# GELU MLP on one core: the first W1 column group plain, W1 cast by GpSimd's queue, W2 through DRAM in fp16

## Chip, core and metric

One core of one Trainium2 chip. The metric is the device time of one execution in microseconds; lower is better. Inputs and output are fp32 in DRAM; the matmuls run in fp16 with fp32 sums in PSUM.

## Reference

```python
x = np.random.randn(16, 512, 768)     # seen as 8192 rows of 768
w1 = np.random.randn(768, 3072); b1 = np.random.randn(3072)
w2 = np.random.randn(3072, 768)

y = np.matmul(x, w1) + b1
y = 0.5 * y * (1.0 + erf(y / np.sqrt(2.0)))
return np.matmul(y, w2)
```

## The kernel before

**Two phases.** Phase 1 computes gelu(x W1 + b1) and stores it in fp16, transposed (hidden column on the partitions), in sixteen DRAM tensors `gd`, one for each 512 rows of x. Phase 2 reads `gd` back, multiplies by W2 and writes the output.

**Plain and fast products.** Both phases use a bilinear scheme of 20 block products where the ordinary product needs 24. The lists at the top (`P1_ORD`, `P1_WOPS`, `P1_XOPS`, `P1_OPS`, and those of `P2`) say which sums of blocks are multiplied and how the products are combined. In phase 1 a unit is one column group of W1 (512 of the 3072 columns, two halves of K by four tiles of 128) times one block of 1536 rows of x (three thirds of 512): 20 products of three matmuls. `w1_ops` makes the 20 operands of one W1 group (sums, differences and signed copies), `x_sums` makes the 13 sums of x of one block. There are five blocks and six groups, so 30 units; `p1_block(b)` runs the six units of one block. While a product is summed in PSUM, ScalarE copies and VectorE adds (L343, L348) take intermediate values out; a Gelu on ScalarE (L497, in `finish`) ends each output tile of 128 x 512, 12 a unit. In phase 2 a unit is 512 rows times all of W2: 20 products of eight matmuls with 384 columns (L873), 16 units.

The first 512 rows of x, which don't fit in blocks of 1536, go through `plain_tile`: six matmuls for one tile of 128 columns (L630), 24 tiles.

**Start.** x's first 512 rows and all six W1 groups come on SP's queue in fp32 (L396, L419) and are cast to fp16 by ScalarE and VectorE; the x tiles are transposed on TensorE (L480, evicted at L486 and L488). The 24 plain tiles follow. Next to three of them (`X1_AT`) GpSimd's queue loads the three thirds of block 0 (L643), with a cast on the way; they too are transposed on TensorE, and then block 0's units begin.

**x of later blocks.** `load_x(b)` has GpSimd's queue cast 256 rows at a time from x to a DRAM copy `xd` in fp16 (L667, six a block), and SP's queue load them with a transposing DMA (L671, six a block). The lists `CAST_AT` and `TR_AT` name the units of the block before behind which they are planned.

**Stores of Gelu.** Each Gelu writes into one of `NGST` = 11 staging slots; a DMA stores it to `gd` (L503: SP's queue, GpSimd's for 16 of the plain tiles), and the slot is free when the store has landed. In phase 2 the same memory holds `NOSB` output slots of 1536 bytes: 7.

**W2.** During the last block of phase 1, GpSimd's queue loads W2 in two halves with a cast (L772, four DMAs each, one buffer for both), and VectorE, GpSimd and ScalarE make the operands (`P2_WOPS`). Eight operands that are plain blocks of W2 are loaded once more, directly to where they stay (L810); these places are free only as the last units of phase 1 finish with W1's operands there.

**What sets the order.** The kernel schedules itself. `S.add` hands a task with its engines and guessed durations, the values that it reads, the buffer it allocates, `after=` (tasks that it is planned behind) and `due=` (a planned time) to `Sched`, which simulates the engines and emits every engine's instructions in the order that the simulation finds. TensorE's order is that of the code. An engine's queue is then worked off in that order, with waits where data or buffers need them.

Of the kernel before, what the change touches and what calls it, by code (L numbers as in the profile page):

```python
# [13 lines left out]
P = 128  # L14
# [24 lines left out]
X1_AT = (9, 12, 15)  # L39
# [213 lines left out]
def kernel(  # L253
# [21 lines left out]
    NS = 18  # L275
# [6 lines left out]
    NGST = 11  # L282
# [11 lines left out]
    xd = drp.tile([R, K], FP16, name="xd")  # L294

    def a16(off, n):
        return ar[:, off // 2: off // 2 + n]
# [4 lines left out]
    def s_off(i):  # L302
        return O_SUM + i * SL
# [50 lines left out]
    ctx.enter_context(tc.manual_schedule())  # L354
    make_identity(nc, ident[:])
# [18 lines left out]
    sums = Pool([s_off(i) for i in (16, 17)], heir=sums_done)  # L374
    xnat = Pool([s_off(14)], heir=lambda t, s: [sums.put(t, s + SL * i) for i in range(2)])
    xtr = Pool([s_off(12)], heir=lambda t, s: [sums.put(t, s + SL * i) for i in range(2)])
    wraw = Pool([s_off(i) for i in range(12)], heir=sums.put)
# [31 lines left out]
    w1load = []  # L409
    for u in range(6):  # L410
        halves = []
        cuts = ((0, 256), (256, 512)) if u == 0 else ((0, 512),)
        raw = [Val(wraw), Val(wraw)]
        done = [[None] * 4 for _ in range(2)]
        for c0, c1 in cuts:
            for i in range(2):
                o = O_WF + (u * 2 + i) * 6144
                f = Val()
                w1load.append(S.add({"SP": 0.45}, lambda e, o=o, i=i, c0=c0, c1=c1, u=u: nc.sync.dma_start(  # L419
                    out=a32(o, 1536).rearrange("p (k c) -> p k c", c=512)[:, :, c0:c1],  # L420
                    in_=w1r[:, 3 * i:3 * i + 3, u * 512 + c0:u * 512 + c1]), makes=[f], work=2.15 * (c1 - c0) / 512))
# [9 lines left out]
        wv.append((raw, done))  # L431
# [14 lines left out]
    def w1_ops(u, due):  # L446
        raw, done = wv[u]
        after = list(x0c) + (w1cast[:4 + 2 * u] if u else [])
# [173 lines left out]
    plain_mm = []  # L622

    def plain_tile(u, q):
        raw, done = wv[u]
        bv = Val(bank)

        def mm(e):
            for kc in range(KC):
                nc.tensor.matmul(out=ps[:, bv.slot, :], lhsT=raw_w1(u, 2 * q + kc // 3)[:, kc % 3, :],  # L630
                                 rhs=a16(x0T.slot + kc * 1024, 512), start=(kc == 0), stop=(kc == KC - 1))
        plain_mm.append(S.add({"PE": 6 * MM1}, mm, reads=[done[0][q], done[1][q], x0T], frees=[x0T, raw[0], raw[1]], alloc=bv))
        return finish(([bv], lambda: ps[:, bv.slot, :]), u * 4 + q, 0, 1, [bv], queue="POOL" if u < 4 else "SP")

    pg = []
    x1n = []
    for u in range(6):
        for q in range(4):
            pg.append(plain_tile(u, q))
            if u * 4 + q in X1_AT:  # L640
                j = len(x1n)
                v = Val()
                S.add({"POOL": 0.8}, lambda e, j=j: nc.gpsimd.dma_start(  # L643
                    out=a16(O_XB + j * 6144, 3072).rearrange("p (s k) -> p s k", k=K), in_=xr[:, 4 + 4 * j:8 + 4 * j, :]),
                    makes=[v], work=5.3, after=[pg[-1]])
                x1n.append(v)
    x1done = []
    for s in range(12):
        j, c = divmod(s, 4)
        pt, dur, ev, bv, dv = transpose_tile(  # L650
            x1n[j], lambda kc, s=s: a16(O_XB + s * 1536 + kc * 256, P),
            lambda j=j, c=c: x_third(0, j)[:, :, c * P:(c + 1) * P], xsv[0][j])
        x1done.append(pt)
        S.add(dur, ev, reads=[bv], makes=[xsv[0][j], xsv[0][3 + j]])
# [5 lines left out]
    def load_x(b):  # L660
        r0 = BLK[b]
        for y in range(6):
# [8 lines left out]
            S.add({"SP": 0.45}, lambda e, a=a, z=z, j=j: nc.sync.dma_start_transpose(  # L671
# [3 lines left out]
    def x_sums(b, due0, dur):  # L675
# [11 lines left out]
        for (d, op, a, z) in sorted(P1_XOPS, key=lambda o: (need[o[0]], o[0])):  # L687
# [4 lines left out]
            def fn(e, fa=fa, fb=fb, v=v, op=op):  # L692
                step = 1536 if e == "DVE" else 512
                for h in range(0, 1536, step):
                    comb(e, a16(v.slot + 2 * h, step), op, fa()[:, h:h + step], fb()[:, h:h + step])
            prev = [S.add({"DVE": dve_tt(1536), "POOL": 3 * pool_tt(512)} if b else {"DVE": dve_tt(1536)}, fn, reads=[va, vb], alloc=v,
                          order=prev, due=due0 + dur * need[d], port=True)]
# [3 lines left out]
    def p1_block(b):  # L701
# [4 lines left out]
        for u in range(6):  # L706
            if b == 0:
                w1_ops(u, S.pe_ideal - 1.0)

# [218 lines left out]
```

## Time and profile before

| | |
|---|---|
| median of 3 runs | 922.49 us (921.5 to 922.61) |
| profiled execution | 921.39 us, span 919.6 us |
| TensorE busy | 861.4 us (94%), 4601 matmuls |
| VectorE, ScalarE, GpSimd busy | 629.1, 430.4, 164.8 us |
| phase 2 matmuls (L873) | 2560, 419.3 us |
| phase 1 fast matmuls (L714) | 1800, 399.2 us |
| plain matmuls (L630) | 144, 33.2 us |
| direct W2 loads (L810), issue to landing | median 20.3 us |
| x casts to DRAM (L667), issue to landing | median 10.9 us |
| mean granted TensorE clock | 0.981 |

Times in the timeline run from the span's start. A row of the timeline has start, duration, engine, line, operation, names and count; in brackets stands the idle time of the engine before it and what ended that. Rows marked SPq are DMA issues, which don't count as busy. A stretch of TensorE's idle time is time that the kernel could lose; idle time of another engine is none in itself.

### The profile page before, as it was taken

The page shows a single profiled execution, that of the slowest core. Times are in us where ns is not written, and L with a number is a line of the kernel's source. Part 1 is how long each engine was busy: PE and PEld are TensorE (multiplying, and loading weights), DVE is VectorE, ACT ScalarE, POOL GpSimd, SP SyncE. Part 2 cuts the span into 40 slices and gives each one's busy share as a digit, 9 for nine tenths or more (in the row PEclk, how much of TensorE's full clock was granted, in tenths as well). Part 3 has the DMA queues.
Part 4 walks back from the last instruction along what each step waited for, and adds up shares of the span by engine and source line. Part 5 has one row for each costly group of instructions (what it writes and reads, how often), then busy time and mean ns, then how long its engine had stood idle before and what let it go on. Part 6 is the DMA issues. An engine that isn't in the chain of part 4 may idle for free.

```text
span 919.6 us, 13541 instructions
## 1 busy us (share of the span) xinstructions
PE 861.4 (94%) x4601; PEld 449.8 (49%) x4601; DVE 629.1 (68%) x1041; ACT 430.4 (47%) x711; POOL 164.8 (18%) x165
## 2 busy tenths in 40 slices
PE   6958999999899999987976999999999999999997
PEld 2433444444344444433433556565666666666664
DVE  4937567565656756678686677777777877777773
ACT  8856786787687768755763111212121111212121
POOL 1400085048007504645130000000000000000000
PEclk9979999999999999999999899999999999999999
DMA  9994747854874785482989655555665555555611
GB/s 336 274 214 120 190 138 160 229 162 146 209 189 144 171 218 161 126 196 73 200 254 297 185 173 185 166 176 169 206 206 191 165 172 190 167 164 190 206 69 69
DMA packets 132793, 166.85 MB, mean 181 GB/s; under 512 B 47580, under 2 KB 121332, under 8 KB 126196
## 3 DMA queue, kind: packets, MB, share of 16 engines
q1 hardware_dynamic: 122144, 144.22, 49.7%
q0 software_dynamic: 10544, 21.76, 12.7%
q8 instruction: 36, 0.59, 0.3%
q14 instruction: 33, 0.27, 0.1%
q10 hardware_dynamic: 36, 0.01, 0.0%
HBM read 100.68 MB, written 84.93 MB: 202 GB/s over the span
## 4 chain that ended last, share of the span: by engine, by line
PE 82%; DMA 7%; DVE 6%; ACT 3%; issue 2%; SPq 0%; POOL 0%; ACTq 0%; DVEq 0%; POOLq 0%
PE ps L873 44%; PE ps L714 35%; DVE ar L343 4%; DMA gd<-ar 4%; DMA ar<-in_w_dram 3%; PE ps L630 2%; DVE vt L343 2%; ACT ar L488 1%; ACT ar L497 1%; ACT ar L348 1%; ACT vt L348 1%; SPq L396 0%; DVE ar L352 0%; SPq L419 0%; ACT L497 0%
## 5 line engine op out<-in xcount | busy, mean ns | idle before, releaser
L873 PE MATMUL ps<-ar 128*128 128x384 f16 x2560 | 419.3, 327 | 8.9 <-DMA ar<-in_w_dram 8.9
L714 PE MATMUL ps<-ar 128*128 128x512 f16 x1800 | 399.2, 383 | 28.0 <-DVE vt L343 19.1
L873 PEld LDWEIGHTS <-ar 128*128 128x128 f16 x2560 | 250.8, 98 | 177.4 <-issue 9.9
L714 PEld LDWEIGHTS <-ar 128*128 128x128 f16 x1800 | 177.1, 99 | 249.9 <-issue 42.1
L343 DVE TENSOR_TENSOR vt<-vt,ps 128x512 f32<-128x512 f32 (+1 forms) x260 | 167.6, 645 | 139.2 <-ACT vt L348 70.4
L343 DVE TENSOR_TENSOR ar<-ar 128x1024 f16<-128x1024 f16 (+2 forms) x385 | 248.9, 674 | 20.2 <-PE ps L873 9.8
L348 ACT ACTIVATE vt<-ps 128x512 f32<-128x512 f32 (+1 forms) x232 | 125.1, 542 | 263.1 <-PE ps L873 238.1
L497 ACT ACTIVATE ar<-vt,b1t 128x512 f16<-128x512 f32 x240 | 166.5, 717 | 93.4 <-DVE vt L343 83.8
L343 DVE TENSOR_TENSOR vt<-ps,vt 128x512 f32<-128x512 f32 (+1 forms) x230 | 147.5, 642 | 77.9 <-ACT vt L348 34.5
L343 POOL TENSOR_TENSOR ar<-ar 128x512 f16<-128x512 f16 (+1 forms) x98 | 129.1, 1352 | 254.5 <-PE ps L714 126.8
L497 ACT ACTIVATE ar<-ps,b1t 128x512 f16<-128x512 f32 x144 | 93.1, 675 | 10.9 <-DMA gd<-ar 9.3
L348 ACT ACTIVATE ar<-vt 128x384 f32<-128x384 f32 x48 | 25.1, 523 | 109.7 <-DVE vt L343 77.9
L630 PE MATMUL ps<-ar 128*128 128x512 f16 x144 | 33.2, 392 | 2.7 <-ACT ar L348 1.7
L341 DVE SCALAR_TENSOR_TENSOR vt<-vt,ps 128x512 f32<-128x512 f32 (+1 forms) x46 | 29.3, 637 | 3.7 <-PE ps L714 0.8
L348 ACT ACTIVATE ar<-ar 128x1536 f16<-128x1536 f32 (+4 forms) x30 | 27.7, 953 | 6.2 <-DMA ar<-in_w_dram 4.9
L343 DVE TENSOR_TENSOR ar<-vt 128x384 f32<-128x384 f32 x48 | 26.8, 559 | 1.7
L630 PEld LDWEIGHTS <-ar 128*128 128x128 f16 x144 | 14.3, 100 | 21.4 <-ACT ar L348 2.8
L341 DVE SCALAR_TENSOR_TENSOR ar<-vt,ps 128x384 f32<-128x384 f32 x16 | 8.9, 554 | 22.0 <-PE ps L873 22.0
L480 PE MATMUL ps<-ident,ar 128*128 128x128 f16 x96 | 9.8, 270 | 10.5 <-DMA ar<-in_x_dram 7.7
L503 POOL DMA_DIRECT2D gd<-ar x16 | 8.8, 556 | 30.6 <-ACT ar L497 30.6
L480 PEld LDWEIGHTS <-ar 128*128 128x128 f16 x96 | 7.5, 120 | 12.7 <-DMA ar<-in_x_dram 8.1
L667 POOL DMA_DIRECT2D xd<-in_x_dram x24 | 11.7, 494 | 5.5 <-DMA ar<-in_x_dram 5.5
(23 smaller groups left out, 57.4 us busy)
## 6 DMA issues: line engine op xcount, KB each, us to landing
ar<-gd SPq DMA_DIRECT2D x48, 1024.0 KB, 5.5
gd<-ar SPq DMA_DIRECT2D x368, 128.0 KB, 1.8
out_dram<-ar SPq DMA_DIRECT2D x128, 192.0 KB, 2.0
xd<-in_x_dram POOLq DMA_DIRECT2D x24, 384.0 KB, 10.9
ar<-in_w_dram SPq DMA_DIRECT2D x10, 768.0 KB, 13.2
ar<-in_w_dram POOLq DMA_DIRECT2D x8, 576.0 KB, 11.4
ar<-in_w_dram POOLq DMA_DIRECT2D x8, 384.0 KB, 20.3
ar<-in_x_dram POOLq DMA_DIRECT2D x3, 768.0 KB, 10.0
```

What stands on the lines that cost most here:

```text
L341: eng.scalar_tensor_tensor(out=o, in0=a, scalar=-1.0, in1=b, op0=ALU.mult, op1=ALU.subtract)
L343: eng.tensor_tensor(out=o, in0=a, in1=b, op=ALU.add if op == "+" else ALU.subtract)
L348: nc.scalar.activation(out=o, in_=a, func=ACTF.Copy, scale=float(sg))
L480: nc.tensor.transpose(out=o[:, kc * P:(kc + 1) * P], in_=nat_ap(kc), identity=ident[:])
L488: nc.scalar.copy(out=dst_fn(), in_=i)
L497: ft = S.add({"ACT": act_ps(512) + 0.02}, lambda e: nc.scalar.activation(out=a16(g.slot, 512), in_=src[1](), func=ACTF.Gelu, bias=b1t[:, t ...
L503: {"SP": nc.sync, "POOL": nc.gpsimd}[e].dma_start(out=gd[un][:, t, :], in_=a16(g.slot, 512))
L630: nc.tensor.matmul(out=ps[:, bv.slot, :], lhsT=raw_w1(u, 2 * q + kc // 3)[:, kc % 3, :], rhs=a16(x0T.slot + kc * 1024, 512), start=(kc == ...
L667: S.add({"POOL": 0.5}, lambda e, a=a: nc.gpsimd.dma_start(out=xd[a:a + 256, :], in_=xf[a:a + 256, :]), makes=[c], work=2.1, after=gate)
L714: nc.tensor.matmul(out=ps[:, bk, :], lhsT=w1_ap(u, w)[:, kt * P:(kt + 1) * P], rhs=xa[:, kt * 512:(kt + 1) * 512], start=(first and kt == ...
L873: nc.tensor.matmul(out=ps[:, bk, 0:NB], lhsT=xa[:, j, :], rhs=a16(w2half[w][j // 4].slot + (j % 4) * W1T, NB), start=(first and j == 0), s ...
```

## The change

- The first W1 group is computed plain for block 0 as well (with all of its rows, so 2048 rows of that group are plain); block 0 keeps five fast units. Groups 1 and 2 are plain for the first 512 rows before the fast units, groups 3 to 5 each just before their own unit.
- Only group 0 of W1 is loaded in fp32 by SP. Groups 1 to 5 are loaded with a cast by GpSimd's queue, two DMAs a group, into four slots that are used again. Block 0's x is loaded by the same queue, in turn with groups 1 and 2.
- W2 is cast into a DRAM copy `w2d` by four DMAs on GpSimd's queue, planned behind units 3 and 4 of blocks 1 and 2. The loads of W2 (both halves and the direct ones) read `w2d` on SP's queue.
- The transposing loads of x are issued by ScalarE's queue.
- All Gelu stores are on SP's queue. There are 8 staging slots (5 output slots in phase 2) instead of 11 (7), and 19 slots for sums instead of 18.
- The due times of the x sums are 4 us earlier, and a Gelu on one element at the very start loads the activation table.

```diff
-    NS = 18
+    NS = 19
-    NGST = 11
+    NGST = 8
+    w2d = drp.tile([H, N], FP16, name="w2d")
...
+    tiny = main.tile([P, 1], FP32, name="tiny")
+    nc.vector.memset(tiny[:], 0.0)
+    nc.scalar.activation(out=tiny[:], in_=tiny[:], func=ACTF.Gelu)
...
+    def w1_load(u, after):
+        raw = [Val(wraw if u else wraw0) for _ in range(2)]
+        done = [[None] * 4 for _ in range(2)]
+        wv.append((raw, done))
+        if u:
+            for i in range(2):
+                S.add({"POOL": 0.8}, lambda e, i=i: nc.gpsimd.dma_start(
+                    out=a16(raw[i].slot, 1536).rearrange("p (k c) -> p k c", c=512),
+                    in_=w1r[:, 3 * i:3 * i + 3, u * 512:u * 512 + 512]), alloc=raw[i], work=2.8, after=after)
+                done[i] = [raw[i]] * 4
+            return
...
+    for j in range(3):
+        if j:
+            w1_load(j, x0c[-2:])
+        v = Val()
+        S.add({"POOL": 0.8}, lambda e, j=j: nc.gpsimd.dma_start(
+            out=a16(O_XB + j * 6144, 3072).rearrange("p (s k) -> p s k", k=K), in_=xr[:, 4 + 4 * j:8 + 4 * j, :]),
+            makes=[v], work=5.3, after=x0c[-2:])
+        x1n.append(v)
+    plain_group(0, xt0, 0)
+    w1_ops(0, S.pe_ideal + 5.0)
+    for j in range(3):
+        for c in range(4):
...
+        if j:
+            plain_group(j, xt0, 0)
+        plain_group(0, (lambda j=j: x_third(0, j), [xsv[0][j]], []), 512 + 512 * j)
+    w1_load(3, x1done[-1:])
...
-            S.add({"SP": 0.45}, lambda e, a=a, z=z, j=j: nc.sync.dma_start_transpose(
+            S.add({"ACT": 0.6}, lambda e, a=a, z=z, j=j: nc.scalar.dma_start_transpose(
...
-                          order=prev, due=due0 + dur * need[d], port=True)]
+                          order=prev, due=due0 + dur * need[d] - 4.0, port=True)]
...
             if b == 0:
+                if u == 0:
+                    blk_units[b].append([x1done[-1]])
+                    continue
                 w1_ops(u, S.pe_ideal - 1.0)
+                if u >= 3:
+                    plain_group(u, xt0, 0)
...
+            if b == 0 and u < 3:
+                w1_load(u + 3, blk_units[0][u][:1])
...
+    w2r = w2d.rearrange("(i j p) n -> p j i n", p=P, j=8)
+    w2dv = [Val()]
+    for i in range(4):
+        S.add({"POOL": 0.8}, lambda e, i=i: nc.gpsimd.dma_start(
+            out=w2d[768 * i:768 * i + 768, :], in_=w2[768 * i:768 * i + 768, :]), makes=w2dv, work=6.2,
+            after=blk_units[1 + i // 2][3 + i % 2][:1])
...
-            S.add({"POOL": 0.8}, lambda e, j=j, hf=hf, rv=rv: nc.gpsimd.dma_start(
+            S.add({"SP": 0.45}, lambda e, j=j, hf=hf, rv=rv: nc.sync.dma_start(
...
-        S.add({"POOL": 0.6}, lambda e, v=v, kg=kg, nh=nh, hf=hf: nc.gpsimd.dma_start(
+        S.add({"SP": 0.45}, lambda e, v=v, kg=kg, nh=nh, hf=hf: nc.sync.dma_start(
```

`plain_group(u, xT, row)` runs `plain_tile` for the four tiles of group u.

## The prediction

> **What bounds the kernel.** I read the page first: TensorE is busy 94% of the span and carries 82% of the chain of waits, so only a stretch in which TensorE idles, or runs at half clock, can be worth anything. The sliced table puts those at the start, at the block changes, and between 390 and 512 us. Busy time by stage (us, then engines, granted clock, DMA share, GB/s):
>
> ```profile
> 50.00:60.00 10.00, 4.75 (x48) 4.18 (x49) 0.35 (x1) 10.00 (x18) 1.44 (x3) 0.56 1.18 253
> 60.00:70.00 10.00, 7.21 (x24) 2.38 (x24) 9.05 (x12) 2.82 (x5) 0.00 (x0) 0.75 0.59 133
> 80.00:146.00 66.00, 66.00 (x307) 29.91 (x306) 41.04 (x61) 50.52 (x83) 26.48 (x24) 1.00 0.56 159
> 417.00:431.00 14.00, 7.68 (x35) 3.35 (x35) 12.40 (x11) 5.68 (x10) 9.95 (x3) 0.97 0.21 69
> 462.00:487.00 25.00, 19.10 (x81) 8.24 (x80) 21.16 (x29) 17.31 (x27) 7.68 (x8) 0.93 0.90 244
> 487.00:512.00 25.00, 16.06 (x82) 8.39 (x80) 12.62 (x21) 4.05 (x8) 0.74 (x1) 0.80 1.00 253
> ```
>
> The first number behind the stretch's length is TensorE: full in 80 to 146, with holes elsewhere. Then the timeline around the holes:
>
> ```profile
> 62.07 4.14 PE L714 MATMUL ps<-ar 128*128 128x512 f16 x12 [2.52 <-DVE ar L343]
> 79.39 5.99 PE L714 MATMUL ps<-ar 128*128 128x512 f16 x27 [0.22 <-DVE ar L343]
> 43.54 1.49 POOL L667 DMA_DIRECT2D xd<-in_x_dram  x3
> 146.97 2.92 POOL L667 DMA_DIRECT2D xd<-in_x_dram  x6
> 162.55 0.72 ACT L497 ACTIVATE ar<-vt,b1t 128x512 f16<-128x512 f32 x1 [3.09 <-DMA gd<-ar]
> 165.57 16.78 PE L714 MATMUL ps<-ar 128*128 128x512 f16 x77 [1.49 <-ACT vt L348]
> 430.60 9.60 PE L714 MATMUL ps<-ar 128*128 128x512 f16 x37 [5.36 <-DVE vt L343]
> 477.12 9.62 PE L714 MATMUL ps<-ar 128*128 128x512 f16 x36 [3.97 <-DVE vt L343]
> ```
>
> To be seen: fast products begin at 62.07 and run without holes only from 79.39. GpSimd issues casts of x at 43.54 though the planner put them behind block 0's first unit (62.07 at the earliest), and six in a row at 146.97 though planned over three units of 13 us. So an `after=` orders the plan but isn't a wait on the chip: GpSimd's queue runs ahead until a real buffer stops it. Then a Gelu waits 3.09 us for a staging slot, and TensorE loses 1.49. Last the DMA queues (packets, MB, share of 16 engines) from 148.5 to 162.5, then from 46 to 54; the stores (L503) issued in 150 to 155; the transposes:
>
> ```profile
> q0 software_dynamic: 190, 2.31, 85.3%
> q1 hardware_dynamic: 716, 0.66, 14.1%
> ```
> ```profile
> q0 software_dynamic: 795, 1.39, 82.9%
> q1 hardware_dynamic: 719, 0.66, 29.3%
> ```
> ```profile
> DMA to landing us min/median/max: 10.8/11.6/12.5
> ```
> ```profile
> L671 SPq DMA_TRANSPOSE ar<-xd x24: 1395/1452/1920, 83.5 to 353.2; - x24
> ```
>
> While DRAM-to-DRAM casts run, GpSimd's packets are 12 KB (2.31 MB/190) and take 1.0 us (85.3% of 16 x 14 us over 190); loads into SBUF have 1.7 KB packets of 0.13 us and share with SP's 0.9 KB packets about one for one (795 to 719). A 128 KB store has 8 packets per engine, so beside casts one store passes in about 8 us, and landing grows from 1.7 to 11.6 us.
>
> **The change, part by part** (minus is faster).
>
> A, start. Plain matmuls go from 144 to 216 and fast ones from 1800 to 1740: 12 more, 2.6 us at 0.2163 (66.85 us for 309), included below. Nothing stands ahead of GpSimd's seven loads but the identity masks (over at 1.64), so at 0.77 us an issue they are out by about 7 us and share the engines with SP's x0 and W1 group 0, packet for packet. Group 0 has 96 packets per engine; at 0.15 to 0.17 us a pair they need 14 to 16 us behind x0 (done at about 8), so the last lands near 22, where its last cast now starts at 12.55. Plain tiles then begin at 16 instead of 10.47 and the second half at 22.6. From there: 132 matmuls x 0.2163 = 28.6, 72 transposes at 1.50 per 24 = 4.5, one eviction wait of 1: first fast product at 56.7. The seven loads are down by about 31, so x isn't waited for again. From 56.7 there remain 1740 + 72 = 1812 matmuls, before at 79.39 1749; the 63 more are 13.6, so 70.3 is the same place: -9. The earlier Gelu table load (1.28 at 13.41) is in this. I take -7.5 because W1's arrival is the weak figure; ends -15 (loads don't meet) and +2 (W1 lands 10 later).
>
> B, W1 operands made within block 0. Three groups at 6.2 us of VectorE (20 outputs of 0.28 to 0.55) raise its 41.0 of 66 to 59.6, 90%. +1.5; ends 0 and +5. That x and W1 casts leave ScalarE costs and gains nothing: TensorE covers it.
>
> C, 24 transposes to ScalarE's queue: 24 x 1.452 = 35 us, in pairs of 2.9 in units that leave ScalarE about 3 of 13 us (50.5 of 66 busy). A pair comes about 4 us into a unit, ahead of the copy that chain 3 needs; 2.9 less the nearest gaps (0.65) eats that copy's 1.8 us of room: 0.45, and some 0.2 at the next unit. Ten pairs (two fall into stalls of D): +6.5. Ends 0 (issue overlaps running work) and +15 (1.25 a pair). SP, relieved, wasn't the bound.
>
> On A and C the Trainium skill speaks against the change. SBUF — State Buffer, section SBUF: two separate sides, says that a DMA issued by GpSimd starves for descriptors while VectorE runs two-port copies, about 3.1 instead of 0.62 us; here x loads were issued beside such copies in 0.76 to 0.78 us each, so by the row A stands; by the rule A would be near 0 and the sum 933. DMA: Bandwidth & Descriptors, section Issuing engines are not separate DMA queues, calls the sequencer time saved by another queue usually small; by that C would be near 0 and the sum 919; by the 1.45 us row it isn't.
>
> D, eight Gelu slots for eleven, and W2 cast to DRAM. The first W2 cast of blocks 1 and 2 is planned at unit 3, behind the six x casts (units 0 to 2) and ahead of the x sums that need unit 3's transposes, so it joins the burst. x casts land 2.06 us apart (152.4 to 162.7, six); three times the rows is 6.2. ScalarE's stop: 3.09, + 2.0 (three Gelus fewer: 157.5 instead of 159.46), + 6.2, - 0.7 for one slot freed on the way = 10.6; TensorE's slack was 3.09 - 1.49 = 1.6, so 9.0, and a half-clock piece after so long a hole 1.7 (as in 462 to 487: 7% of 25): 10.7 less 1.5 = 9.2 in each of two blocks. Block 3 has no W2 cast: +1. The second W2 casts lie among the sums: 6.2 us at a Gelu in 1.07 us need 6 of 8 slots: 0. D = +19.4; ends +3 (the casts lie apart) and +26 (the second ones join too, part covered). Output staging falls from 7 to 5 slots: stores land in 2.0 us and come 1.3 apart: 0, without that cover +3.
>
> E, x sums due 4 us earlier: holes after VectorE at the four block starts, 5.6 in all (0.96, 0.95, 0.96, 2.76); I take -2.5, ends -5.6 and +1.
>
> F, W2 from DRAM in fp16 by SP. Holes: 6.4 before 430.6, 5.9 around 477, 8.9 in 487 to 512, and half clock 3.4 + 2.5: 27. The direct loads took 23 us to land beside GpSimd's own; as plain loads behind 1 MB reads on SP's queue (5.5 us) they are in by 497, about when they are needed: -8. The second half's load, down at 461, follows the first half's operations as before but lands some 10 earlier, so its operations spread: -4, not all, since VectorE stays at 85%. The first hole is VectorE blocked behind GpSimd's sums (2.7 us for 0.95), which stay: -2. F = -14; ends -24 and -5 (SP waits for the W2 buffer with stores queued behind it, which fill eight slots).
>
> Sum: -7.5 + 1.5 + 6.5 + 19.4 - 2.5 - 14 = +3.4. The profiled execution took 921.39 (span 919.6), 1.1 under the median: 924.8 there, **925.9** against 922.49.
>
> **Rivals.** (1) Faster: the casts lie apart from the x casts, D is +3: 925.9 - 16.4 = 909.5. For it: planned gates keep them two units away; against: six x casts ran in a row. It decides once D is under 14. (2) Faster: the start's loads don't meet and the transition closes fully, A -13, F -22: 912. For it: TensorE is idle for loads in both places; against: the packet sharing. (3) Slower still: W1 group 0 starves and ScalarE's pairs hit harder, A 0, C +13: 940. (4) The transition's wait only moves to SP, F -5: 935, the change then not doing what it says there.
>
> **Numbers.** Forecast 0.34, rivals 0.22, 0.17, 0.17, 0.10. The forecast's own range is 921 to 931. A difference under 0.2% (1.85 us) can't be told from none. Faster: 0.39 + 0.02 of the forecast's low end = 0.41; same 0.10; slower 0.22 + 0.27 = 0.49. The range, 907 to 939, reaches to rivals 1 and 3 and leaves out about 0.2.
>
> **What will show it.** A: GpSimd's loads at 2 to 7 us, first fast product at 55 to 59. D: Gelus waiting some 10 us for `gd` in blocks 1 and 2 behind a row of seven casts. C: transposes of 1.4 us or more on ScalarE with holes of half a microsecond after them. F: TensorE's holes in 390 to 512 at half of 27. Without D's waits I am wrong and the kernel is faster; if fast products start after 62, slower.

## The result, and the profile after

The changed kernel took **945.4 us** (median of 4 runs, 944.71 to 951.5) against 922.08 for the kernel before beside it (4 runs, 921.5 to 922.61): ratio 1.0268, 95% interval 1.0225 to 1.0311. It is slower, by more than the forecast of 925.9 and its range (907 to 939) said. The profiled execution has a span of 943.66 us, 24.05 more than before.

Cutting both traces at the same matmuls gives the bill. The columns are us; a fast unit without holes takes 12.95, a block of six 77.7. A unit counts from its first matmul to the next unit's first.

| stage | before | after | difference |
|---|---|---|---|
| first plain matmul at | 10.47 | 14.27 | |
| first fast product at | 62.07 | 60.82 | |
| start to block 1 | 146.07 | 150.14 | +4.1 |
| block 1 | 81.01 | 96.67 | +15.7 |
| block 2 | 80.93 | 98.03 | +17.1 |
| block 3 | 80.01 | 79.31 | -0.7 |
| block 4 | 98.55 | 94.99 | -3.6 |
| phase 2, unit 0 | 38.04 | 27.49 | -10.6 |
| phase 2, other 15 units | 390.16 | 392.09 | +1.9 |

The same stages after the change, as windows (start:end, length, TensorE busy, weight loads, VectorE, ScalarE, GpSimd, granted clock, DMA share, GB/s), block 1 to block 3:

```profile
150.14:246.81 96.67, 82.33 (x361) 36.14 (x360) 53.81 (x79) 58.26 (x95) 20.61 (x23) 0.91 0.73 182
246.81:344.84 98.03, 81.11 (x362) 35.77 (x360) 57.63 (x84) 59.43 (x96) 19.59 (x21) 0.91 0.71 175
344.84:424.15 79.31, 79.31 (x361) 35.64 (x360) 53.09 (x79) 60.33 (x98) 14.16 (x12) 0.98 0.56 160
```

Blocks 1 and 2 hold the loss: TensorE is busy 82.33 of 96.67 us, 14.3 of holes; and 82.33 against 77.7 without loss, at a granted clock of 0.91, is another 4.6 of slower matmuls. What stands in the holes is seen in the timeline of the changed kernel around block 1's start (start, duration, engine, work; in brackets the idle time before and what ended it):

```profile
145.33 2.97 POOL L686 DMA_DIRECT2D xd<-in_x_dram  x6
148.29 1.02 POOL L791 DMA_DIRECT2D w2d<-in_w_dram  x2
160.55 0.69 ACT L509 ACTIVATE ar<-ps,b1t 128x512 f16<-128x512 f32 x1 [10.15 <-DMA gd<-ar]
161.78 6.70 PE L738 MATMUL ps<-ar 128*128 128x512 f16 x18 [8.23 <-ACT vt L348]
173.09 1.95 ACT L509 ACTIVATE ar<-vt,b1t 128x512 f16<-128x512 f32 x3 [10.40 <-DMA gd<-ar]
174.59 3.70 PE L738 MATMUL ps<-ar 128*128 128x512 f16 x10 [6.11 <-DVE vt L343]
```

GpSimd issues all six x casts and then **both** W2 casts of the block in 4 us. Two Gelus wait 10 us each for a store to free a slot, and TensorE loses 8.23 and 6.11. The stores (L515) issued between 147 and 152:

```profile
DMA to landing us min/median/max: 23.9/25.4/26.2
```

The DMA queues from 150 to 172 (packets, MB, share of 16 engines; q0 is GpSimd's, q1 SP's):

```profile
q0 software_dynamic: 273, 3.98, 88.2%
q1 hardware_dynamic: 646, 0.60, 8.4%
```

The casts' packets are 14.6 KB on average (3.98 MB / 273) and hold the engines for 88% of the time; the stores' 1 KB packets get 8%. A store that took 1.7 us elsewhere takes 25.

Block 0 lost in its first units, in the timeline:

```profile
57.26 1.99 POOL L686 DMA_DIRECT2D xd<-in_x_dram  x4
60.82 7.93 PE L738 MATMUL ps<-ar 128*128 128x512 f16 x36
64.32 5.50 ACTq L690 DMA_TRANSPOSE ar<-xd  x1
69.95 3.42 ACTq L690 DMA_TRANSPOSE ar<-xd  x1
71.37 1.23 PE L738 MATMUL ps<-ar 128*128 128x512 f16 x3 [2.61 <-DVE vt L343]
74.73 1.86 PE L738 MATMUL ps<-ar 128*128 128x512 f16 x4 [2.13 <-ACT vt L348]
```

Two transposing loads occupy ScalarE's queue for 5.50 and 3.42 us, not 1.45, while four x casts run; the holes follow them. In blocks 1 to 3, where they meet no casts, the units that hold them take 12.95 to 13.16.

### The profile page after: what moved, and what is told of

Same layout as the page of the kernel before. It is cut to its first block, busy times and chain, and to the rows that moved or that the text cites. A ratio compares the mean times of both kernels' runs of the same rounds, so it can differ in the third digit from the quotient of the medians.

```text
span 943.7 us, 13433 instructions
## 1 busy us (share of the span) xinstructions
PE 869.1 (92%) x4613; PEld 452.4 (48%) x4613; DVE 631.2 (67%) x1026; ACT 416.7 (44%) x711; POOL 118.8 (13%) x109
## 3 DMA queue, kind: packets, MB, share of 16 engines
q0 software_dynamic: 6608, 20.45, 11.6%
## 4 chain that ended last, share of the span: by engine, by line
PE 78%; DMA 12%; DVE 5%; issue 2%; ACT 1%; ACTq 1%; SPq 0%; DVEq 0%
PE ps L904 42%; PE ps L738 31%; DMA gd<-ar 7%; PE ps L640 5%; DMA ar<-gd 3%; DVE vt L343 2%; DMA ar<-in_w_dram 2%; DVE ar L343 2%; ACTq L690 1%; ACT ar L509 1%; PE ps L492 1%; ACT vt L348 0%; DVE ar L352 0%; SPq L400 0%; SPq L430 0%
## 5 line engine op out<-in xcount | busy, mean ns | idle before, releaser
L738 PE MATMUL ps<-ar 128*128 128x512 f16 x1740 | 391.6, 387 | 46.9 <-ACT vt L348 21.9
L343 DVE TENSOR_TENSOR ar<-ar 128x1024 f16<-128x1024 f16 (+2 forms) x395 | 257.3, 676 | 33.3 <-DMA ar<-gd 10.9
L343 DVE TENSOR_TENSOR vt<-vt,ps 128x512 f32<-128x512 f32 (+1 forms) x254 | 163.3, 644 | 108.8 <-PE ps L738 48.8
L343 DVE TENSOR_TENSOR vt<-ps,vt 128x512 f32<-128x512 f32 (+1 forms) x225 | 144.4, 642 | 111.2 <-ACT vt L348 46.5
L509 ACT ACTIVATE ar<-vt,b1t 128x512 f16<-128x512 f32 x232 | 161.1, 717 | 92.4 <-DVE vt L343 66.3
L343 POOL TENSOR_TENSOR ar<-ar 128x512 f16<-128x512 f16 (+1 forms) x60 | 94.1, 1602 | 294.5 <-PE ps L738 141.5
L509 ACT ACTIVATE ar<-ps,b1t 128x512 f16<-128x512 f32 x152 | 99.9, 675 | 51.2 <-DMA gd<-ar 38.8
L640 PE MATMUL ps<-ar 128*128 128x512 f16 x216 | 52.2, 400 | 9.3 <-ACT ar L348 5.3
L348 ACT ACTIVATE ar<-ar 128x384 f16<-128x384 f16 (+3 forms) x36 | 19.9, 569 | 12.9 <-DMA ar<-in_w_dram 10.7
L420 POOL DMA_DIRECT2D ar<-in_w_dram x10 | 7.6, 764 | 86.6 <-ACT ar L509 49.7
```

What stands on the lines that cost most here:

```text
L343: eng.tensor_tensor(out=o, in0=a, in1=b, op=ALU.add if op == "+" else ALU.subtract)
L348: nc.scalar.activation(out=o, in_=a, func=ACTF.Copy, scale=float(sg))
L420: S.add({"POOL": 0.8}, lambda e, i=i: nc.gpsimd.dma_start(out=a16(raw[i].slot, 1536).rearrange("p (k c) -> p k c", c=512), in_=w1r[:, 3 * ...
L509: ft = S.add({"ACT": act_ps(512) + 0.02}, lambda e: nc.scalar.activation(out=a16(g.slot, 512), in_=src[1](), func=ACTF.Gelu, bias=b1t[:, t ...
L738: nc.tensor.matmul(out=ps[:, bk, :], lhsT=w1_ap(u, w)[:, kt * P:(kt + 1) * P], rhs=xa[:, kt * 512:(kt + 1) * 512], start=(first and kt == ...
```

## The experiments

All times of blocks below are from the profiled execution; "lost" is what blocks 1 to 3 took over 3 x 77.7. Block 0 without holes takes 77.7 in the kernel before and 80.5 after the change (372 matmuls x 0.2163). The ratio is to runs of the kernel before that were made beside each run; their medians lay between 918.73 and 924.54, so totals of different experiments compare better by ratio. One arrangement was traced twice (w1_first turned out to repeat the changed kernel): "lost" was 40.9 and 44.2, so a difference of some 3 us in that column shows little.

| run | median us | ratio to before (95%) | block 0 | 1 | 2 | 3 | lost |
|---|---|---|---|---|---|---|---|
| before | 922.08 | | 84.0 | 81.0 | 80.9 | 80.0 | 8.9 |
| after | 945.4 | 1.0225-1.0311 | 89.3 | 96.7 | 98.0 | 79.3 | 40.9 |
| w2_apart | 946.3 | 1.0195-1.0386 | 97.8 | 90.3 | 90.8 | 88.4 | 36.4 |
| rows_apart | 932.13 | 1.0074-1.0199 | 90.5 | 91.9 | 86.5 | 80.3 | 25.5 |
| w2_rows_apart | 936.89 | 1.0100-1.0276 | 90.7 | 90.8 | 94.1 | 79.2 | 31.0 |
| transposes_on_sp | 948.01 | 1.0247-1.0371 | 83.1 | 104.5 | 96.5 | 79.9 | 47.7 |
| spread | 932.74 | 1.0085-1.0177 | 85.7 | 86.3 | 90.5 | 86.0 | 29.7 |
| w2_spread | 940.84 | 1.0181-1.0257 | 89.3 | 90.2 | 89.6 | 88.1 | 34.7 |
| before_8_slots | 940.64 | 1.0153-1.0281 | 85.2 | 83.9 | 84.5 | 82.2 | 17.5 |
| w2_late | 951.16 | 1.0160-1.0502 | 90.2 | 90.1 | 85.0 | 89.3 | 31.3 |
| eleven_slots | 939.46 | 1.0112-1.0217 | 90.5 | 94.2 | 91.0 | 80.5 | 32.6 |
| eleven_spread | 932.69 | 1.0043-1.0149 | 85.7 | 91.6 | 89.0 | 85.9 | 33.4 |
| eleven_rows | 932.04 | 1.0043-1.0124 | 90.4 | 92.1 | 83.6 | 82.0 | 24.5 |
| w1_first | 945.5 | 1.0145-1.0315 | 89.4 | 96.9 | 100.4 | 79.9 | 44.2 |
| eleven_w2spread | 925.29 | 1.0024-1.0074 | 90.1 | 82.8 | 86.1 | 85.2 | 21.0 |
| eleven_w2spread_sp1 | 917.58 | 0.9954-0.9994 | 80.8 | 83.4 | 88.6 | 84.8 | 23.7 |
| eleven_w2spread_sp1_w1first | 914.41 | 0.9899-0.9957 | 80.3 | 84.0 | 86.4 | 86.5 | 23.7 |
| before_scalar_transposes | 923.79 | 1.0015-1.0057 | 85.7 | 80.3 | 81.0 | 80.7 | 8.9 |
| x_in_threes | 919.83 | 0.9957-0.9990 | 80.3 | 89.1 | 88.8 | 86.8 | 31.6 |
| x_in_pairs | 918.42 | 0.9965-1.0000 | 80.3 | 88.0 | 87.0 | 86.1 | 28.1 |

**1. The W2 casts moved out of the run.**

```diff
-            after=blk_units[1 + i // 2][3 + i % 2][:1])
+            after=xst[1 + i][2:3])
```

(`xst[b]` holds the sums of block b in their order.)

> Change: the four W2 casts are planned behind sums of x, one in each of blocks 0 to 3, so that in GpSimd's queue each stands behind six sums and no longer behind the six x casts. Theory (the burst of eight casts keeps the eight Gelu slots waiting): blocks 1 and 2, 96.7 and 98.0 us after the change, fall to 79 to 84 each; a W2 cast alone (6.2 us) stops a Gelu for at most some 3 us in each of blocks 0 to 3; total 912 to 920. Rival 1 (eight slots are too few for the six x casts by themselves): blocks 1 and 2 stay above 90, total above 933. Rival 2 (the W2 casts cost their DMA time wherever they stand): the loss spreads over blocks 0 to 3, total 938 to 946.

Measured: 946.3, no gain. The four W2 casts now stand apart. One cost 0.7 us in block 1's last unit (13.65), two cost 4 in the last units of blocks 2 and 3 (17.1 and 17.0). In block 0 the third stretch grew by 8.0 (19.33 to 27.36); no Gelu waited for a slot there, but two transposing loads on ScalarE took 6.74 and 3.35 us beside the cast. Issue to landing was, for the four:

```profile
DMA to landing us min/median/max: 9.1/10.8/11.5
```

That is 10.8 us beside stores, not the 6.2 scaled from the x casts, and eight slots cover 8.6 (8 x 1.07, an estimate). The x run alone still cost the first units 11.7, 9.0 and 6.6. The theory fell; rival 1's signs were met (blocks 1 and 2 above 90, total above 933), and rival 2's total all but met.

**2. Shorter packets.** In rows_apart both DRAM copies, in w2_rows_apart the W2 copy alone:

```diff
-    xd = drp.tile([R, K], FP16, name="xd")
-    w2d = drp.tile([H, N], FP16, name="w2d")
+    xd = drp.tile([R, K + 64], FP16, name="xd")
+    w2d = drp.tile([H, N + 64], FP16, name="w2d")
```

> Change: the rows of both DRAM copies are 64 elements further apart, so that the cast of 256 or 768 rows is no longer one contiguous piece and its packets should shrink from 12 KB to about one row (1.5 KB); bytes and order stay. Theory (a 12 KB packet holds an engine about 1 us for each packet of a Gelu store that it alternates with, so stores starve): stores land in 3 to 5 us instead of 24 to 26 beside the casts, Gelu waits for gd fall under 2 us, blocks 1 and 2 to 79 to 81 each, and the transposing loads of block 0 that took 5.5 and 3.4 us to issue fall to 1.5; total 903 to 912. Rival (the DMA engines are simply full, whatever the packets): waits stay at 7 to 10 us, total 940 to 947, or worse if short packets are slower in themselves.

> Change: the rows of the W2 copy alone are 64 elements further apart; the x copy keeps its 12 KB packets. Theory (stores starve behind long packets): the six x casts still stop the eight slots, as eleven were stopped before by about 3 us a block, the two W2 casts behind them no longer: blocks 1 and 2 at 83 to 87 each, total 920 to 930. Rival (the eight slots are the cause, not the W2 casts): blocks 1 and 2 above 92, total above 936.

Measured: 932.1 and 936.9. The DMA queues of rows_apart from 150 to 172:

```profile
q0 software_dynamic: 2211, 3.25, 82.2%
q1 hardware_dynamic: 2036, 1.86, 31.6%
```

and its stores issued from 155 to 172:

```profile
DMA to landing us min/median/max: 8.5/10.6/11.1
```

Packets of 1.5 KB alternate with the stores' about one for one (2211 to 2036), so the stores move three times as much (1.86 MB for 0.60), and a store lands every 1.47 us. That is still slower than a Gelu each 1.07 (six Gelus in a row wait 0.64 to 0.80 us each), and the casts of x now land 2.67 us apart instead of 1.95. But most of what block 1 loses is something else: its second unit takes 23.04, 10.1 too long, where two transposing loads met W2's casts and held ScalarE for 4.74 and 3.65 us. So packet length is part of the cause (13 us of the total), and what is left is of both kinds. rows_apart lies between its theory and its rival; w2_rows_apart missed its 920 to 930 and reached its rival's total, but only one of the rival's two blocks. The Trainium skill (DMA: Bandwidth & Descriptors, section Queues, rings and completion order) has each DMA engine change queues only at whole packets; both kernels agree: from 150 to 160 the changed kernel passed 160 packets of q0 and 158 of q1, long for short, and here it is 2211 to 2036. Block 0 gained nothing: the transposing loads still took 5.18 and 4.53.

**3. The transposing loads back on SP.**

```diff
-            S.add({"ACT": 0.6}, lambda e, a=a, z=z, j=j: nc.scalar.dma_start_transpose(
+            S.add({"SP": 0.45}, lambda e, a=a, z=z, j=j: nc.sync.dma_start_transpose(
```

> Change: the transposing loads of x are issued by SP's queue again, all else as after the change. Theory (on ScalarE they cost in block 0 alone, where they are issued while x casts run): the three unit stretches of block 0 that are 9.0 us too long come back by 7 to 9 us, blocks 1 to 3 are unchanged within 2 us, total 935 to 939. Rival 1 (the forecast's term: 0.65 us for each pair on a full ScalarE): about 6.5 us spread over all blocks, total 939. Rival 2 (the loss in block 0 is not the issue on ScalarE but the late x of block 1 or the crowded VectorE): block 0 stays, or SP's queue with its stores is held and it becomes longer, total 943 to 950.

Measured: block 0 came back by 6.2 us, a little less than the theory's 7 to 9, but block 1 grew by 7.8: total 948. That is rival 2's total, but its reason, stores held behind the loads on SP, isn't seen: between 166.3 and 241 no Gelu waits for a slot. Of the 7.8, 6.4 lie in block 1's last two units (14.49 and 17.81), where the casts for block 2 are already issued at 230.4, 17 us ahead of that block, and a Gelu waits 4.44.

**4. All casts spaced, and W2's alone.** `hold` writes a mark on ScalarE and has GpSimd copy it ahead of the cast:

```diff
+        S.add({"ACT": 0.22}, lambda e, k=k: nc.scalar.copy(out=mark[:, k:k + 1], in_=tiny[:]), after=[at], makes=[m])
+        S.add({"POOL": 0.2}, lambda e, k=k: nc.gpsimd.tensor_copy(out=held[:], in_=mark[:, k:k + 1]), reads=[m], makes=[h])
...
-    for i in range(4):
+    for i in range(12):
...
-            after=blk_units[1 + i // 2][3 + i % 2][:1])
+            after=hold(blk_units[1 + i // 6][3 + i % 6 // 2][10 * (i % 2)]))
```

> Change: the W2 copy is made in twelve casts of 256 rows, and each of these and each x cast (but the first two of block 1's x) stands in GpSimd's queue behind a one-element copy of a mark that ScalarE writes at the start or in the middle of a unit; so no two casts are closer than half a unit (6.5 us), bytes unchanged. Theory (an unbroken run of casts keeps every store from landing, and eight slots cover some 9 us of Gelus; a run of 2 us is covered): Gelus wait for gd under 1 us each, stores land in under 5 us, blocks 1 to 3 at 78 to 81 each instead of 96.7, 98.0 and 79.3, total 903 to 912. Rival 1 (the casts cost TensorE their DMA time wherever they stand, as W2's casts seemed to when they were moved apart): blocks 1 and 2 above 88, total above 930. Rival 2 (the marks and holds themselves cost: ScalarE and GpSimd have no room): units 1 to 6 each longer by half a us or more, total 915 to 930.

> Change: only W2 is cast in twelve spaced pieces (units 4 to 6 of blocks 1 and 2); the six x casts stay in one run. Theory (length of the run decides): the last units of blocks 1 and 2 lose nothing, the first units keep what the x run alone costs with eight slots (between 1.6 and 11.7 us, the two values seen so far): blocks 1 and 2 at 80 to 91 each, total 912 to 932. Rival (DMA time wherever it stands): 4 us for each 768 rows remain, blocks 1 and 2 above 88 and total above 930.

Measured: 932.7 and 940.8. In spread the waits for `gd` are down to 2.1 us and yet blocks 1 to 3 take 86 to 90: x casts now run when the transposing loads are issued, and these took 3.27, 2.86 and 2.49 us in block 3. In w2_spread the last three units of block 1 take 13.5, 12.96 and 12.95, those of block 2 14.62, 13.79 and 12.95: spaced in 256 rows, W2's casts cost 0.6 and 2.5 us there, where the rival had 4 us for each 768 rows. Both totals lie in the ranges of the rivals ("wherever they stand"), but W2's casts don't bear them out: in w2_spread 31.5 of the 34.7 lost lie in the first units of the three blocks, beside the x run.

**5. The slots alone, in the kernel before; and no W2 copy after the change.** The first is `NGST = 8`; the second loads W2 by GpSimd as before:

```diff
-    NGST = 11
+    NGST = 8
```

```diff
-            S.add({"SP": 0.45}, lambda e, j=j, hf=hf, rv=rv: nc.sync.dma_start(
+            S.add({"POOL": 0.8}, lambda e, j=j, hf=hf, rv=rv: nc.gpsimd.dma_start(
```

> Change, made on the kernel before: eight Gelu slots (and five output slots) instead of eleven (seven), nothing else. Theory (a run of six x casts, 12.4 us, is what eight slots don't cover): the Gelu waits of 3.1 us at each block's start grow by 2 to 8 us, blocks 1 to 3 (81.0, 80.9, 80.0) become 83 to 90 each, total 926 to 945. Rival 1 (three Gelus fewer, 2.0 us in each of three blocks, part covered): 924 to 928. Rival 2 (slots don't matter without W2's casts): 921 to 924.

> Change: W2 isn't cast to DRAM; its halves and direct blocks are loaded with a cast by GpSimd's queue during the last block, as in the kernel before; all else as after the change. Theory (runs of casts on eight slots): blocks 1 and 2 keep the x run's share, 80 to 90 each instead of 96.7 and 98.0; the stretch from block 4 through the first unit of phase 2 gives back the 14.1 us that the change gained there; total 925 to 943. Rival (W2's casts account for all of it): blocks 1 and 2 at 79 to 80.5, total 923 to 926.

Measured: 940.6, within the theory's range, and 951.2 (two runs, 944.64 and 957.67), above the theory's 925 to 943. Eight slots cost the kernel before 20 us, 11 of them at its start (first fast product at 73.14; a Gelu there waits 9.51) and 8.6 in blocks 1 to 3. Without any W2 copy the changed kernel still loses 31.3 in blocks 1 to 3. Its timeline at block 1's start (151.09):

```profile
146.27 2.97 POOL L685 DMA_DIRECT2D xd<-in_x_dram  x6
162.81 0.69 ACT L508 ACTIVATE ar<-ps,b1t 128x512 f16<-128x512 f32 x1 [11.47 <-DMA gd<-ar]
164.03 6.25 PE L737 MATMUL ps<-ar 128*128 128x512 f16 x17 [9.55 <-ACT vt L347]
```

Six x casts, not eight, and still a wait of 11.47. They are issued 4.8 us ahead of the block; in the kernel before (and in before_8_slots) 0.9 after its start. Block 4 and phase 2's first unit took 130.7 together, 8.2 more than after the change.

**6. Eleven slots.** Room comes from one slot for sums fewer, with the transposed first rows in W1 group 5's place:

```diff
-    NS = 19
+    NS = 18
-    NGST = 8
+    NGST = 11
-    xtr = Pool([s_off(6)], heir=lambda t, s: [sums.put(t, s + SL * i) for i in range(2)])
+    xtr = Pool([O_W1 + 109 * W1T])
...
+                if u == 4:
+                    last_plain = plain_group(5, xt0, 0)
```

Three runs: this alone, with all casts spaced as in 4, and with the short packets of 2.

> Change: eleven Gelu slots (seven output slots) again, room for them by 18 slots for sums, with the transposed first 512 rows kept where W1 group 5's operands come later (its plain tiles move up to unit 5); casts and transposes stay as after the change. Theory (what decides is the run of casts against the slots): three more slots cover 3.2 us of each stall of 7 to 10 us, the 25 us run of eight casts still outlasts them: blocks 1 and 2 at 85 to 93 instead of 96.7 and 98.0, total 924 to 938. Rival 1 (the slots account for nearly all of D, as eight slots alone cost the kernel before 20 us): blocks 1 and 2 at 84 or less, total 920 or less. Rival 2 (with a run this long slots hardly matter): blocks 1 and 2 above 94, total above 939.

> Change: eleven slots as in the run beside it, and all casts in spaced pieces of 256 rows. With eight slots the spaced casts left blocks 1 to 3 at 86.3, 90.5 and 86.0, with few waits for gd (2.1 us twice) but transposing loads of 2.5 to 5 us of issue on ScalarE, now that casts run beside them. Theory 1 (slots): the remaining loss was of slots, blocks 1 to 3 at 78 to 81, total 900 to 910. Theory 2 (the remaining loss is ScalarE held by transposing loads that take twice as long beside casts): the waits for gd vanish but blocks 1 to 3 stay at 83 to 88, total 915 to 928.

> Change: eleven slots, and the rows of both DRAM copies 64 elements further apart (short packets), casts in runs as after the change. With eight slots and short packets a store landed every 1.47 us beside the casts, and blocks 1 and 2 took 91.9 and 86.5. Theory (a run of 31 us brings 29 Gelus; 21 stores land in it, and eleven slots cover the rest, eight don't quite): no Gelu waits for gd, blocks 1 to 3 at 78 to 81 each, total 903 to 913. Rival (the DMA engines' total is short, slots only shift the wait): blocks 1 and 2 above 84, total above 920.

Measured: 939.5, 932.7 and 932.0. Slots alone give back 8.3 us of the 40.9, a little less than the theory said (total 924 to 938) and far less than rival 1; the total is just inside rival 2's. eleven_spread has almost no waits for `gd` (the longest is 1.92) and no smaller loss than spread: theory 2's mechanism, ScalarE held by transposing loads, though it put blocks 1 to 3 at 83 to 88 and they took 86 to 92. eleven_rows missed its 903 to 913, but not by slots. In block 1 the timeline puts a wait of 7.59 down to a store; in it ScalarE's queue stood at a transposing load:

```profile
172.87 3.77 ACTq L690 DMA_TRANSPOSE ar<-xd  x1
177.02 0.72 ACT L509 ACTIVATE ar<-vt,b1t 128x512 f16<-128x512 f32 x1 [7.59 <-DMA gd<-ar]
```

The next load took 3.79, and the unit that holds the two 24.13. As in rows_apart, they met W2's casts.

**7. W1 ahead of GpSimd's loads, first try.**

```diff
+    S.add({"POOL": 0.2}, lambda e: nc.gpsimd.tensor_copy(out=hold[:], in_=a32(O_WF + 6144 + 256 * 4, 1)), reads=[w1f[-1]], frees=[],
+          makes=[])
```

> Change: GpSimd copies one element of W1 group 0's last fp32 piece before it issues its loads, so that x's first rows and W1 group 0 have the DMA engines to themselves; all else as after the change. Theory (GpSimd's loads, issued at 1.65 to 7.1, halve the rate of SP's: group 0 complete at 24.4 and the first plain matmul at 14.3): the first plain matmul at 10 to 11, group 0 complete at 11 to 14, GpSimd's loads 8 to 10 us later, the first fast product at 56.5 to 59 instead of 60.8, total 940 to 943 (or up to 2 us longer if x's thirds then come late). Rival (VectorE and ScalarE's work sets the start, not the loads): the first fast product at 60 to 62, total 944 to 947.

Inconclusive: the planner put four of the seven loads ahead of the copy, W1 landed at 24.7 as after the change, and the run repeats that kernel (945.5).

**8. Eleven slots and spaced W2, then the transposing loads of block 1 on SP, then W1 first.** In the last, `w1here` is what GpSimd's copy of one element of W1 group 0's last piece makes; all seven loads stand behind it:

```diff
+            S.add({"SP": 0.45} if b == 1 else {"ACT": 0.6}, lambda e, a=a, z=z, j=j: (nc.sync if b == 1 else nc.scalar).dma_start_transpose(
...
-            makes=[v], work=5.3, after=x0c[-2:])
+            makes=[v], work=5.3, after=w1here.prods)
```

> Change: eleven slots, W2 cast in twelve spaced pieces in the last three units of blocks 1 and 2 (where neither x casts nor transposing loads run), the six x casts in one run as after the change, transposing loads on ScalarE. Theory (an unbroken run of eight casts was D; with the run at six and eleven slots the kernel before lost 3.3 us a block): blocks 1 to 3 at 80 to 83 each instead of 94.2, 91.0 and 80.5 with eleven slots alone, block 0 unchanged at 90, total 915 to 921. Rival (W2's 25 us of DMA time cost TensorE wherever they stand): blocks 1 and 2 above 86, total above 924.

> Change: as the run beside it with eleven slots and spaced W2, and the six transposing loads for block 1 alone on SP's queue (in block 0 they meet x casts), those of the later blocks on ScalarE. Theory (C is the issue of a transposing load, 3.4 to 5.5 us on ScalarE while x casts run, 1.4 to 1.9 else): block 0 shorter by 5 to 8 us than with all on ScalarE, blocks 1 to 3 the same within 1.5 us, total 908 to 915. Rival (on SP they hold the stores behind them, as in the run with all of them on SP, where block 1 lost 7.8): no gain within 2 us.

> Change: as the run beside it, and all seven loads of GpSimd at the start stand behind a copy of one element of W1 group 0's last piece (in the run w1_first the loads were issued ahead of that copy, so it changed nothing there). Theory (the loads halve the rate of SP's): group 0 complete at 11 to 14 instead of 24, the first plain matmul at 10 to 11 instead of 14.3, the first fast product 2 to 4 us earlier than in the run beside it, total 2 to 4 less. Rival 1 (x's thirds, 10 us later, are then what the start waits for): the first fast product at 60 to 66, total the same or up to 4 more. Rival 2 (VectorE and ScalarE set the start): no difference within 1 us.

Measured: 925.3, 917.6 and 914.4. The first missed its 915 to 921: the loss fell from 32.6 to 21.0, not to the 8.9 of before. The second shows C: block 0 went from 90.1 to 80.8, no loss left (its total still missed 908 to 915). On SP's queue the same two loads also took longer, but TensorE ran on:

```profile
60.73 19.64 PE L754 MATMUL ps<-ar 128*128 128x512 f16 x88
62.19 2.70 SPq L701 DMA_TRANSPOSE ar<-xd  x1
71.33 3.50 SPq L701 DMA_TRANSPOSE ar<-xd  x1
```

The third shows A, in its timeline:

```profile
12.61 0.30 POOL L664 COPY first<-ar 128x1 f32<-128x1 f32 x1 [10.97 <-DMA ar<-in_w_dram]
12.85 0.93 POOL L672 DMA_DIRECT2D ar<-in_x_dram  x1
```

W1 group 0 is complete at 12.56 instead of 24.4, and fast products start at 53.70 instead of 60.73: 7.0 us. Of these 3.2 are left in the total; block 3 and the transition are longer.

**9. ScalarE's queue alone, in the kernel before** (the edit of 3 the other way round, with `nc.scalar`).

> Change, made on the kernel before: its transposing loads are issued by ScalarE's queue, nothing else (part C of the change alone). There they are issued from 83.5 on, after the x casts have landed. Theory (C costs where casts run beside it, and nothing else): issue times 1.4 to 2 us, blocks 1 to 3 at 79 to 81.5 instead of 81.0, 80.9 and 80.0, total 917 to 922. Rival (the forecast's term, 0.65 us a pair on a full ScalarE): units 2 to 4 of each block longer by 0.4 us or more, total 925 to 930.

Measured: 923.8, 1.5 to 5.7 thousandths over before and just above the theory's 917 to 922; blocks 1 to 3 lose 8.9, as before. All 24 loads (ns, min/median/max):

```profile
L671 ACTq DMA_TRANSPOSE ar<-xd x24: 1370/1547/2183, 87.6 to 357.2; - x24
```

They come after the casts have landed there, and none takes more than 2.2 us. There is no term of 0.65 a pair.

**10. The x run broken up.** In place of one run of six, GpSimd waits for marks in the block's first unit:

```diff
-            gate = [blk_units[b - 1][CAST_AT[y]][0]]
+            if b > 1:
+                if y in {0: 2, 3: 14}:
+                    held_x = hold(blk_units[b - 1][0][{0: 2, 3: 14}[y]])
+                gate = held_x
```

> Change: as the run with eleven slots, spaced W2, block 1's transposing loads on SP and W1 first; and the x casts of blocks 2 to 4 stand behind marks of ScalarE in two runs of three (third and fifteenth product of the block's first unit), no longer in one run of six right behind W2's last piece. In that run blocks 2 and 3 took 86.3 and 86.5, with waits for gd of 2.2 and 2.9 in their first units. Theory (the unbroken run of casts against the slots): runs of 6.2 us are covered by eleven slots, the first units of blocks 2 and 3 at 14 to 15.5 instead of 19.4 and 21.2, total 900 to 907. Rival (the casts' DMA time comes back elsewhere, as stores or transposing loads that are later): the loss moves to units 2 and 3, total 910 to 915.

> Change: as the run beside it, with the x casts of blocks 2 to 4 in three runs of two (second, ninth and sixteenth product of the block's first unit). Theory: already runs of three are covered, so no more than 1.5 us less than in the run beside it; or up to 2 more where the last pair, some 2 us later, meets the first transposing loads on ScalarE. Rival (the run's length still costs at 6.2 us): 3 us or more less than the run beside it.

Measured: 919.8 and 918.4, slower than without. The rival's mechanism holds, with more loss than its 910 to 915: first units fall to 13.84 in blocks 2 and 3, second units rise to 20 and 21. The timeline of x_in_threes in block 1's second unit:

```profile
153.97 1.45 POOL L707 DMA_DIRECT2D xd<-in_x_dram  x3 [0.62 <-issue]
155.61 4.54 ACTq L711 DMA_TRANSPOSE ar<-xd  x1
160.34 3.29 ACTq L711 DMA_TRANSPOSE ar<-xd  x1
161.75 0.81 PE L764 MATMUL ps<-ar 128*128 128x512 f16 x3 [1.78 <-DVE vt L343]
164.98 7.31 PE L764 MATMUL ps<-ar 128*128 128x512 f16 x27 [2.42 <-ACT vt L348]
```

The same picture as block 0 after the change: later casts meet the transposing loads, ScalarE stands for 7.8 us, TensorE has two holes.

## Why the prediction was wrong, step by step

**A, start: -7.5 forecast, -4.8 measured** (60.82 plus 372 x 0.2163 is 141.3, against 146.07). The mechanism was right, GpSimd's loads came at 1.65 to 7.1; group 0 landed at 24.4 where the step had it near 22, and fast products began at 60.8, not 56.7. Holding the loads back gave 7.0 more at that point. VectorE's first cast begins at 7.62, after the last of the seven issues (7.1), so this start doesn't test the starving beside VectorE's copies that the prediction weighs against A.

**B, VectorE crowded: +1.5 forecast.** With block 1's transposing loads on SP, block 0 takes 80.8 of an ideal 80.5: at most 0.3.

**C, transposing loads: +6.5 forecast, +9.0 measured, by another mechanism.** The step spread 0.65 a pair over ten pairs. Without casts beside them the loads cost nothing measurable (experiment 9, blocks 1 to 3 after). All 9.0 lie in block 0 (its first three stretches: 7.3, 0.5, 1.2); the 7.3 are where two loads meet x casts. SP in that block gave back 9.3 (90.1 to 80.8).

**D: +19.4 forecast, +32.1 measured** in blocks 1 to 3 (E's share is in it). **This is the step that failed**, in two terms. The first: "The second W2 casts lie among the sums: 6.2 us at a Gelu in 1.07 us need 6 of 8 slots: 0." They did not lie there: GpSimd's queue had both directly behind the x casts, so one run of eight casts that landed from 150.1 to 172.8. The prediction had itself read that an `after=` is no wait on the chip, and took the plan's place for these casts even so; GpSimd's first sum of block 1, which was to stand between them, starts 69.4 us into the block (50.6 in the kernel before). And had they lain there, the price wasn't 0: a W2 cast alone took 10.8 us to land and cost 0.7, 4 and 4 in three last units. The end kept for that case, +26, was also short. The second: the + 2.0 for three Gelus fewer, and the +1 for block 3, price six x casts on eight slots at 1 to 2 us a block. Without any W2 cast (w2_late) blocks 1 to 3 take 22.4 more than before.

What the runs give for the 32.1, in two orders:

- eleven slots instead of eight: 8.3 (40.9 to 32.6); then W2 spaced and out of the run: 11.6 (32.6 to 21.0); 12.1 remain over the kernel before (21.0 to 8.9), 1.8 of them in block 1, 1.4 of which in its fourth unit, where transposing loads meet W2's pieces, and 5.1 in each of blocks 2 and 3, where W2's last piece stands directly ahead of the six x casts;
- or, with eight slots, no W2 casts: 9.6 (40.9 to 31.3); of the 22.4 that remain, 8.6 is what eight slots cost the kernel before; the other 13.8 no run takes apart.

With eight slots, what the first unit loses goes with **where the run stands**. The forecast let it start as before, 0.9 us after the block's start. In every run of the changed kernel with its x casts in one run it starts 3 to 17 us ahead, among the last Gelus of the block before: in w2_late eight stores are issued from 147.1 to 151.9 and all are caught; in the kernel before, nine took from 147.2 to 157.1. Why it starts earlier can be read from GpSimd's queue, before and after: the x casts are issued as GpSimd's last sum of x ends. The planner gave it 24 pieces of sums (512 columns each) in block 0 before and 6 after, 24 and 15 in blocks 1 and 2:

```profile
133.64 13.39 POOL L343 TENSOR_TENSOR ar<-ar 128x512 f16<-128x512 f16 x12 [3.66 <-issue]
138.66 6.72 POOL L343 TENSOR_TENSOR ar<-ar 128x512 f16<-128x512 f16 x6 [37.30 <-DVE ar L343]
```

They end at 147.03 and 145.38, and the casts follow at 146.97 and 145.33 (block 1 starts at 146.07 and 150.14; a sum's end is only roughly known). The first unit then loses about what the run still needs after the block's start: the last x cast landed 11.8, 11.1, 4.2 and 0.6 us after it and the unit lost 12.1, 11.6, 6.6 and 1.6 (w2_late blocks 1 and 3, w2_apart block 3, after block 3). Three cases don't fit: w2_late block 2 (12.2 and 7.3), and w2_spread blocks 2 and 3, with W2's last piece ahead of the run (14.9 and 9.4, 14.4 and 10.4). With eleven slots the early start by itself costs nothing that can be seen: in block 1 of eleven_w2spread the six casts start 6.5 us ahead, and the first two units lose 3.7 where the kernel before loses 3.3. So this is read across runs, not shown by one: a run with the x casts put back to 0.9 was not made, nor one with E's 4 us alone undone, which would say whether E's due times took the sums from GpSimd. That stays open.

**E: -2.5 forecast.** No gain is seen: block 3's first unit took 14.56 after and 14.61 before. No run isolates it.

**F: -14 forecast, -14.1 measured** (block 4 -3.6, phase 2's first unit -10.6). Loading W2 as before gave back 8.2 of it. **Output slots: 0 forecast, +1.9 measured**; gone with seven slots, but five slots in before_8_slots cost nothing either, so its cause is open.

Over the stages that is -4.8 (A) + 8.9 (block 0 over its ideal: B and C) + 32.1 (D and E) - 14.1 (F) + 1.9 = 24.0, against 24.05 between the spans.

Of the rivals, (3) named the right two places, W1's arrival and harder pairs, but priced D as the forecast did; that its 940 came nearest is luck, as A was -4.8 where it had 0, C 9.0 where it had 13, and D 12.7 above its price. Rival (1), casts apart, was tried in w2_apart: 946, not 909.

**The version that beats both** has eleven slots, W2's copy in spaced pieces, block 1's transposing loads on SP and W1 ahead of GpSimd's loads: 914.41, ratio 0.9928 (0.9899 to 0.9957) to the kernel before, so 0.4 to 1.0% less.

## What to carry to other kernels

A DRAM-to-DRAM cast is priced by what it keeps from landing: count the buffers against the whole unbroken run in the issuing queue, read from the emitted order and not from the plan's gates, and against when in the consumer's rhythm it starts. Moving such a run moves the loss along with it where something else that is sensitive, here transposing loads on a compute engine's queue, stands in the new place. A planned order that no data enforces is no order; here it let both W2 casts of a block, and later W2's last spaced piece, join the x run (experiment 8). And where the profile names a store as what a Gelu waited for, look at what the engine's own queue held meanwhile: in eleven_rows it was a transposing load.

## What the runs showed of the hardware

- The issue of a transposing DMA held its engine's queue for 1.37 to 2.18 us where no cast ran beside it (24 loads on ScalarE, before_scalar_transposes). Beside casts on GpSimd's queue it often took much longer: on ScalarE up to 5.50 (after) and 6.74 (w2_apart), on SP 2.70 and 3.50 (eleven_w2spread_sp1), and 5.11 beside two W1 loads (x_in_pairs).
- While casts in 12 to 15 KB packets run, stores stop almost entirely and then land together, some 0.35 us apart (w2_apart: eight issued from 154.6 to 159.3 landed from 170.4 to 172.7).
- Seven loads on GpSimd's queue doubled the time that the four W1 pieces on SP's took from issue to landing (median 15.1 us; 7.7 with the loads held back): the last was there at 24.4, held back at 12.56.
